# Three column groups of the second token group's right parts are made beside the last attention blocks, kept in DRAM and loaded past the branch

## The chip, the cores and the metric

The kernel runs on one core of one Trainium2 chip. The core has five engines that run their own instruction lists in order and wait for each other through semaphores: TensorE (PE, matmuls; PEld is its weight load), VectorE (DVE), ScalarE (ACT), GpSimd (POOL) and SyncE (SP), which here issues every DMA. The metric is device time in microseconds (us) for one execution of the whole program.

## The reference, cut to what matters

One decoder layer over 2048 tokens of width 1024: a modulated input goes through one projection; half of the heads do sparse attention (an indexer picks 256 causal keys for each query), the other half a gated short convolution; both are normalised, concatenated and multiplied with `w_out`; a residual and a LayerNorm follow. Then the feed-forward part, in which this change lies:

```python
def swiglu(h, w_gate, w_up, w_down):
    return (jax.nn.silu(h @ w_gate) * (h @ w_up)) @ w_down

    x = layer_norm(DEEPNORM_ALPHA * x + g1[:, None, :] * mix, ln1_g[l], ln1_b[l])
    ff = swiglu(modulate(x, sh2, sc2), w_gate[l], w_up[l], w_down[l])
    x = layer_norm(DEEPNORM_ALPHA * x + g2[:, None, :] * ff, ln2_g[l], ln2_b[l])
```

`w_gate` and `w_up` are 1024 x 2816, `w_down` 2816 x 1024. The output is 2048 x 1024, float32.

## The kernel before

**Attention.** The 2048 tokens are 16 blocks of 128. `attention` takes them in the order `ORDER = [2, 4, 7, 0, 10, 1, 9, 3, 8, 5, 6, 11, 13, 12, 15, 14]`. A block of number b has b + 1 steps. In each step TensorE makes two 128 x 512 banks of logits (L888 to L890), ScalarE turns each into `p32` and `ph` (L894, L895), GpSimd makes the remainder `pr = p32 - ph` in two pieces (L897), and two steps later TensorE multiplies `ph` and `pr` with the values (L907 to L909). When a block is done, `finish` normalises it and `mix` multiplies it with `w_out` (L947), normalises (`z`, L951 to L957), stores `z` as `xn_d`, transposes it (L965), scales it into `h2` (L968) and stores that as `h2_d`; the steps of `mix` are spread over the following block. A background generator gets one call in each step.

**The feed-forward product** uses Strassen's scheme with seven products, m = 1, 2, 6, 5, 7, 3, 4 (`HM`), in this order. Each product needs a right part (of the tokens, `HT[grp][m]`) and a left part (of the weights). Tokens are two groups, blocks 0 to 7 and 8 to 15. A right part of a group has four column groups i = 0 to 3; column group i comes from blocks 8 grp + i and 8 grp + 4 + i. `prep_h(grp)` makes them: for each i it loads four 256 KB pieces `hr` of `h2_d`, forms the seven combinations (`right`, L1102 to L1114), and splits each into a float16 high part on ScalarE (L1170) and a low part on VectorE or GpSimd (L1171). For group 1 the combinations of m = 7, 5, 6 and the low parts of m = 7, 5, 6, 4 are VectorE's; the combination of m = 4 and the low parts of m = 1, 2, 3 are GpSimd's.

**What lies where.** `late_topk`, then the weights of pair 0 (`prep_w(0, W0, ...)`) and `prep_h(0)` run as the background of the attention; four of the seven parts of group 0 go through a ring of two tiles (`outs`) to DRAM (`t_d`) and are loaded as the attention's buffers come free (L1295). At the attention's end `head` runs products m = 1, 2, 6, 5 of group 0, pair 0. Then all engines pass a branch (L1348, L1349): a flag made on the chip decides whether a general top-k and the whole attention are done again; on these inputs they are not. Behind the branch: the last left parts of pair 0 (m = 4), products 7, 3, 4 of group 0, and, called after the first of these, `second = prep_h(1)` in full. Then group 1, pair 0, whose product m = 1 needs `HT[1][1]` with all four column groups; then ten more pairs, and the down product.

The framework's scheduler decides, from its own estimate of times, in which order the instructions of each engine stand. SP's list is in order too: a store that waits holds back every DMA behind it.

Of the kernel before, what the change touches and what calls it, by code (L numbers as in the profile page):

```python
# [3 lines left out]

# [8 lines left out]
F16 = mybir.dt.float16  # L13
# [8 lines left out]
P = 128  # L22
# [5 lines left out]
CH = 512  # L28
# [34 lines left out]
ORDER = [2, 4, 7, 0, 10, 1, 9, 3, 8, 5, 6, 11, 13, 12, 15, 14]  # L63
# [7 lines left out]
HM = (1, 2, 6, 5, 7, 3, 4)  # L71
# [71 lines left out]
def body(ctx: ExitStack, tc: tile.TileContext, A, out, force=False):  # L143
    nc = tc.nc
    V, S_, G, T = nc.vector, nc.scalar, nc.gpsimd, nc.tensor
    dma = nc.sync.dma_start

    def dram(name, shape, dt):
        pool = ctx.enter_context(tc.tile_pool(name="d_" + name, bufs=1, space=DRAM))
        return pool.tile(shape, dt, name=name)  # L150
# [6 lines left out]
    xn_d = [dram(f"xn_d{b}", [P, D], F32) for b in range(NB)]  # L157
    h2_d = [dram(f"h2_d{b}", [P, KT * P], F32) for b in range(NB)]
    t_d = {m: dram(f"t_d{m}", [P, 2, 4, CH], F16) for m in HM[3:]}
    g_d2 = [{m: dram(f"gg_d{g}_{m}", [P, 4, NP, 2, P], F16) for m in HM} for g in range(2)]  # L160


# [636 lines left out]


    wo = [], []

    def out_weights(pool):
        for x, tag in ((0, "hi"), (1, "lo")):
# [16 lines left out]
    def attention(pool=None, background=None, at_block=None, at_end=None):  # L821
# [104 lines left out]
        def mix(b, on, x, mc):  # L926
            yield
            pt = mbank()
            for k in range(4):
                T.transpose(pt[:, k * P:(k + 1) * P], on[:, 2 * k:2 * k + 2].rearrange("p h d -> p (h d)"), ident)  # L930
            ah = ap.tile([P, 4, P], F16, tag="ah", name=f"ah{b}", bufs=two)
            al = ap.tile([P, 4, P], F16, tag="al", name=f"al{b}", bufs=two)
            p4 = pt.rearrange("p (k t) -> p k t", t=P)
            S_.activation(ah, p4, AF.Copy)
            V.tensor_tensor(al, p4, ah, op=ALU.subtract)
            yield
            z = ap.tile([P, D], F32, tag="z", name=f"z{b}", bufs=1)
            st = ap.tile([P, 2, 6], F32, tag="st", name=f"st{b}", bufs=2)
            for hh in range(2):
                ns = slice(hh * CH, (hh + 1) * CH)  # L940
                ps = mbank()
                n = 0
                for k in (4, 5, 6, 7, 0, 1, 2, 3):
                    hi = ah[:, k] if k < 4 else mc[:, k - 4, 0]
                    lo = al[:, k] if k < 4 else mc[:, k - 4, 1]
                    for a, w in ((hi, wo[0]), (hi, wo[1]), (lo, wo[0])):
                        T.matmul(ps, a, w[k // 4][:, k % 4, ns], start=n == 0, stop=n == 3 * KT - 1)  # L947
                        n += 1
                    if k % 2:
                        yield  # L950
                V.scalar_tensor_tensor(z[:, ns], x[:, ns], ALPHA * WS, ps, op0=ALU.mult, op1=ALU.add)  # L951
                V.bn_stats(st[:, hh], z[:, ns])
            mv = ap.tile([P, 2], F32, tag="mv", name=f"mvl{b}", bufs=2)
            V.bn_aggr(mv, st.rearrange("p a b -> p (a b)"))
            rs = ap.tile([P, 1], F32, tag="rs", name=f"rs{b}", bufs=2)
            root(ap, rs, mv[:, 1:2], 1.0, EPS * WS * WS)
            V.tensor_scalar(z, z, mv[:, 0:1], rs, op0=ALU.subtract, op1=ALU.mult)  # L957
            dma(xn_d[b], z)
            yield
            yield  # L960
            h2 = ap.tile([P, KT, P], F32, tag="h2", name=f"h2_{b}", bufs=1)
            for hh in range(2):
                ps = mbank()
                for k in range(4):
                    T.transpose(ps[:, k * P:(k + 1) * P], z[:, (hh * 4 + k) * P:(hh * 4 + k + 1) * P], ident)  # L965
                for k in range(4):
                    kk = hh * 4 + k
                    S_.activation(h2[:, kk], ps[:, k * P:(k + 1) * P], AF.Identity, scale=sa[:, kk:kk + 1],  # L968
                                  bias=sb[:, kk:kk + 1])
                yield  # L970
            dma(h2_d[b], h2.rearrange("p k t -> p (k t)"))
            yield

        MIXN = 15
# [42 lines left out]
        for i in range(len(steps) + lag):  # L1017
            if i < len(steps):
                p, b, kt = steps[i]
                left = b - kt  # L1020
                if kt == 0:
# [9 lines left out]
                    x = ap.tile([P, D], F32, tag="x", name=f"x{b}", bufs=keep)  # L1031
# [12 lines left out]
            if i < len(steps):  # L1044
# [3 lines left out]
                if near is not None:  # L1048
# [3 lines left out]
                    k = min(n, near[1]) if near[0] is not None else 0  # L1052
# [19 lines left out]
            pass  # L1072
        at.close()

    late = [None]
    ff = ctx.enter_context(ExitStack())

# [37 lines left out]
    RIGHT = (1, 7, 5, 6, 2, 4, 3)  # L1115
# [33 lines left out]

    HT = [{}, {}]  # L1150

    def prep_h(grp):

        for i in range(4):
            b = []
            for k in range(2):
                for t in range(2):
                    x = raws(f"hr{grp}{i}{t}{k}")
                    dma(x, h2_d[grp * 8 + t * 4 + i][:, k * CH:(k + 1) * CH])
                    b.append(x)  # L1160
            y = sums(f"yh{grp}{i}")
            for m in RIGHT:
                x = right(V if grp and m in H1V else G, b, y, m)
                kept = HT[grp].get(m)
                if kept is None:
                    o = outs(f"ht{grp}{i}_{m}").rearrange("p a x t -> p (a x t)").rearrange("p (x n) -> p x n", x=2)
                    hi, lo = o[:, 0], o[:, 1]
                else:
                    hi, lo = (kept[:, z, i].rearrange("p k t -> p (k t)") for z in range(2))
                S_.activation(hi, x, AF.Copy)  # L1170
                (G if grp and m in H1G else V).tensor_tensor(lo, x, hi, op=ALU.subtract)  # L1171
                if kept is None:
                    dma(t_d[m][:, :, i], o)
                yield

    def held_h(pool, grp, ms):
# [108 lines left out]
    def unsettled(bank_):  # L1285
        for _ in ahead:
            pass
        heads["u"] = [temps(f"u{x}") for x in range(2)]
        heads["g"] = prods("g11")
        held_h(early_h[0].enter_context(tc.tile_pool(name="fel", bufs=1, side="right", reuse_waits="tile")), 0, HM[3:])  # L1290
        few = few_s.enter_context(tc.tile_pool(name="few", bufs=1, side="right", reuse_waits="tile"))
        heads["v"] = [few.tile([P, CH], F32, name=f"v{x}") for x in range(2)]
        wring.add(few, 4)
        for m in HM[3:]:
            dma(HT[0][m].rearrange("p x a k t -> p (x a k t)"), t_d[m].rearrange("p x a n -> p (x a n)"))  # L1295
        for _ in prep_w(0, W0, (7, 3), ((0, 0), (1, 0), (1, 1)), {3: (0, 1)}):
            pass
        heads["c"] = heads["g"], sums("c11")
        return flags(bank_)
# [13 lines left out]
    for t in range(4):  # L1313
        for c in range(NCH):
            if c == 1 and t < 3:
                wcs.append(load_wc(t + 1, wca if t % 2 else vp, lambda: vp.tile([P, CH], F32, tag="cr", name="cr", bufs=3)))
            g = conv(c, t, *hts[c], *wcs[t])
            for j in range(3):
                if (t, c, j) == EARLY_ATT:
                    pull(100000)  # L1320
                    scoring.close()
                    a0 = tks.enter_context(tc.tile_pool(name="a0", bufs=1, side="right", reuse_waits="tile"))
                    tc_ = tks.enter_context(tc.tile_pool(name="tc_", bufs=1, side="right", reuse_waits="tile"))
                    late[0] = late_topk(tc_)
                    ahead = after_late()
                    att = attention(a0, ahead, at_block, unsettled)
                    next(att)
                    weights = out_weights(a0)
                    for _ in weights:
                        pass  # L1330
                next(g)
                if j == 0 and prev is not None:
                    for _ in prev:
                        pass
                pull(PULL)
                next(ada, None)
            prev = g
# [5 lines left out]
    front.close()  # L1343
    for _ in att:
        pass


    rv = nc.values_load(fi[0:1, 0:1], min_val=0, max_val=1)  # L1348
    with tc.If(rv > 0):  # L1349
        general_topk(tc, A, s_d, u_d)  # L1350
        for _ in attention():
            pass
        for _ in prep_h(0):
            pass
        with tc.tile_pool(name="ps2", bufs=1, space=PSUM) as ps2:
            for _ in head(lambda: ps2.tile([P, CH], F32, tag="f", name="f", bufs=4)):
                pass
# [10 lines left out]
    held_h(fp, 1, HM)  # L1368
    for r, n in ((wring, 2), (raws, 2), (sums, 2), (temps, 6), (prods, 4), (outs, 4)):
        r.add(fp, n)  # L1370
    for _ in prep_w(0, W0, (4,), ((1, 1),)):
        pass
    Ws = W0
# [35 lines left out]
    fo = [None]  # L1409
    gpool = [None]  # L1410
    pwd = prep_wd()
    second = prep_h(1)
    for p in range(NP):
        nxt = {}
        pw = prep_w(p + 1, nxt) if p + 1 < NP else iter(())
# [90 lines left out]
    for q in range(8):  # L1506
# [11 lines left out]
        for m in HM:  # L1518
# [18 lines left out]
            k = {2: 0, 7: 3, 3: 1, 4: 2}.get(m)  # L1537
            if k is not None:
                b, hh = blocks[k // 2], k % 2
                if (q, m) != (7, 4):  # L1540
                    x = residual(b, hh)
# [93 lines left out]
```

## Time and profile before

| | |
|---|---|
| median of the three runs | 2543.98 us (2542.55 to 2549.05) |
| the profiled execution | 2544.64 us, of which the trace's span is 2542.8 us |
| PE busy | 2319.4 us, 91% of the span |
| DVE, ACT, POOL busy | 1804.2, 1185.0 and 1230.5 us |
| granted TensorE clock, mean | 0.962 of full speed |

Read the span as stages: projections, indexer and convolution to about 900 us, the attention to about 1240, the end of the attention with `head` to the branch at about 1266, the feed-forward pairs from 1269 to 2073, the down product to the end. An engine's busy time beside a wait of another engine in the same stretch says who sets the pace there; a busy share over the whole span does not.

### The profile page before, as it was taken

To read this page: it belongs to the slowest core of one execution; us is meant where nothing else is said; L and a number is where in the kernel's file an instruction comes from. 1 tells how busy PE (TensorE), PEld (TensorE's weight loads), DVE (VectorE), ACT (ScalarE), POOL (GpSimd) and SP (SyncE) were. 2 spreads that over 40 slices of the span, in tenths; PEclk is the share of its full clock that TensorE was granted. 3 is DMA by queue.
4 is the path that set the end of the run, shared out by engine and by line. 5 is a ranking of instruction groups with operands and counts; after the bars stand their busy time and mean duration, and the time that the engine had idled before them with its cause. 6 is when DMAs were issued, how large, how long until landed. Compare 5 with 4: busy or idle time off the path is not lost.

```text
span 2542.8 us, 38397 instructions
## 1 busy us (share of the span) xinstructions
PE 2319.4 (91%) x13538; PEld 1119.3 (44%) x13538; DVE 1804.2 (71%) x3649; ACT 1185.0 (47%) x2263; POOL 1230.5 (48%) x1232
## 2 busy tenths in 40 slices
PE   5799999996879699889969999999999986999998
PEld 3444444443444355555424444444444432444443
DVE  8998999989999876763396666776666697422223
ACT  3687776646767566777543233332333343110000
POOL 3000000003655666898376556655655565855455
PEclk9799999998989899999979999999999998999999
DMA  8421442434131322330242223222222236444443
GB/s 272 127 104 68 149 133 89 150 123 144 58 121 60 126 93 81 117 110 29 106 132 88 75 87 92 84 71 75 71 88 79 85 115 207 150 141 148 128 137 121
DMA packets 213917, 281.72 MB, mean 111 GB/s; under 512 B 15825, under 2 KB 128849, under 8 KB 212945
## 3 DMA queue, kind: packets, MB, share of 16 engines
q1 hardware_dynamic: 213712, 279.17, 34.5%
q8 instruction: 107, 1.75, 0.3%
q14 instruction: 98, 0.79, 0.1%
HBM read 183.20 MB, written 95.91 MB: 110 GB/s over the span
## 4 chain that ended last, share of the span: by engine, by line
PE 35%; POOL 6%; DMA 4%; DVE 3%; issue 2%; ACT 0%; SPq 0%; DVEq 0%; POOLq 0%
PE f L1207 30%; PE f L1503 5%; DMA x<-xn_d 2%; POOL z L1480 1%; DMA gi<-gg_d 1%; POOL x L1491 1%; POOL x L1490 1%; POOL z L1547 1%; POOL z L1548 1%; DMA wd<-in_wd 1%; DVE wdo L216 0%; DVE h L1171 0%; DVE z L1536 0%; POOL wd L1112 0%; POOL yd L1105 0%
## 5 line engine op out<-in xcount | busy, mean ns | idle before, releaser
L897 POOL TENSOR_TENSOR pr<-p,ph 128x256 f16<-128x256 f32 x544 | 379.6, 730 | 140.2 <-ACT ph L895 61.2
L1207 PE MATMUL f<-h,wwg 128*128 128x512 f16 x1800 | 419.9, 383 | 25.0 <-ACT h L1170 18.0
L1207 PE MATMUL f<-h,wwu 128*128 128x512 f16 x1800 | 414.1, 380 | 0.0
L1241 POOL TENSOR_TENSOR go<-g,go 128x512 f16<-128x512 f32 x126 | 169.7, 1356 | 274.1 <-ACT go L1240 236.3
L1503 PEld LDWEIGHTS <-gi 128*128 128x128 f16 x1848 | 180.7, 99 | 276.2 <-DMA gi<-gg_d 47.4
L1207 PEld LDWEIGHTS <-wwg 128*128 128x128 f16 x1848 | 182.1, 99 | 232.3 <-issue 14.9
L1207 PEld LDWEIGHTS <-wwu 128*128 128x128 f16 x1848 | 181.1, 98 | 234.2 <-issue 17.0
L1503 PE MATMUL f<-wdo,gi 128*128 128x512 f16 x1032 | 242.1, 386 | 15.6 <-DMA gi<-gg_d 6.8
L865 DVE CUSTOM_DVE_ANT_0 jk<-m,ua 128x512 bf16<-128x512 f32 (+3 forms) x320 | 193.7, 605 | 56.2 <-PE m L863 41.6
L894 ACT ACTIVATE p<-l 128x512 f32<-128x512 f32 x272 | 158.3, 598 | 90.7 <-PE l L890 69.2
L1240 ACT ACTIVATE go<-g 128x512 f16<-128x512 f32 x132 | 82.5, 627 | 230.6 <-issue 82.8
L447 ACT ACTIVATE r<-xs 128x512 f32<-128x512 f32 (+3 forms) x304 | 153.4, 548 | 57.3 <-PE xs L446 14.0
L895 ACT ACTIVATE ph<-p 128x512 f16<-128x512 f32 x272 | 166.5, 635 | 2.9
L909 PE MATMUL o<-vst,pr 128*128 128x65 f16 x1088 | 140.4, 196 | 14.4 <-POOL pr L897 13.7
L1503 PE MATMUL f<-wdr,gi 128*128 128x512 f16 x576 | 136.5, 386 | 16.2 <-DMA gi<-gg_d 16.1
L737 PE MATMUL b<-hi,wch 128*128 128x512 f16 x384 | 146.7, 382 | 0.0
L737 PE MATMUL b<-lo,wch 128*128 128x512 f16 x384 | 146.3, 381 | 0.0
L737 PE MATMUL b<-hi,wcl 128*128 128x512 f16 x384 | 146.3, 381 | 0.0
L907 PE MATMUL o<-vst,ph 128*128 128x65 f16 x1088 | 142.8, 194 | 1.8 <-ACT ph L895 1.8
L908 PE MATMUL o<-vst,ph 128*128 128x64 f16 x1088 | 141.5, 194 | 0.0
L1470 ACT ACTIVATE frs<-fmv,epsw 128x1 f32<-128x1 f32 x16 | 4.7, 294 | 282.3 <-DVE fmv L1467 282.3
L863 PE MATMUL m<-k1T,qst 128*128 128x512 f16 (+3 forms) x320 | 105.4, 360 | 29.5 <-DVE mp L865 26.0
(384 smaller groups left out, 5194.3 us busy)
## 6 DMA issues: line engine op xcount, KB each, us to landing
gg_d<-go SPq DMA_DIRECT2D x154, 256.0 KB, 2.6
gi<-gg_d SPq DMA_DIRECT2D x112, 256.0 KB, 3.0
wa<-in_w_ada SPq DMA_DIRECT2D x64, 256.0 KB, 2.9
wg<-in_wg SPq DMA_DIRECT2D x49, 256.0 KB, 3.0
wu<-in_wu SPq DMA_DIRECT2D x49, 256.0 KB, 3.0
wd<-in_wd SPq DMA_DIRECT2D x44, 256.0 KB, 3.0
gi<-gg_d SPq DMA_DIRECT2D x56, 192.0 KB, 2.8
wa<-in_w_ada SPq DMA_DIRECT2D x16, 512.0 KB, 8.6
```

The lines of the kernel that those rows point to most:

```text
L447: S_.activation(r[:, i:i + e], ps[:, 0:e], AF.Relu)
L737: T.matmul(ps, w[:, k, j * P:(j + 1) * P], x[:, k], start=n == 0, stop=n == 3 * KT - 1)
L865: V.tensor_tensor_reduce(jk[:, 0:w], ps[:, 0:w], u[:, j * 512:j * 512 + w], scale=1.0, scalar=-3e38, op0=ALU.add, op1=ALU.max, accum_out=m ...
L894: S_.activation(p32, pl_, AF.Exp, scale=DH ** -0.5)
L895: S_.activation(ph, p32, AF.Copy)
L897: G.tensor_tensor(pr[:, i:i + CH // 2], p32[:, i:i + CH // 2], ph[:, i:i + CH // 2], op=ALU.subtract)
L907: T.matmul(o, lhs, vst[:, kt, 64:129], start=kt == 0 and hh == 0, stop=False)
L908: T.matmul(o[:, 0:64], lhs, vst[:, kt, 0:64], start=False, stop=False)
L909: T.matmul(o, pr[:, hh * P:(hh + 1) * P], vst[:, kt, 64:129], start=False, stop=kt == b and hh == 3)
L1207: T.matmul(ps, w[:, x, k * P:(k + 1) * P], h[:, y, :, k], start=n == 0, stop=n == 11)
L1241: (V if (p, grp) in LASTG else G).tensor_tensor(o[:, :, 1], x4, o[:, :, 0], op=ALU.subtract)
L1503: T.matmul(ps, g[:, p - p0, x], wd_tiles[m, p][:, y], start=p == 0 and n == 0, stop=p == NP - 1 and n == 2)
```

## The change

`prep_h` takes the list of column groups that it makes. A generator `other = prep_h(1, H1PARTS)` with `H1PARTS = [1, 0, 3]` joins the attention's background behind the first one. A set `mixed` holds the blocks whose `h2` has been stored; a column group is begun only when both of its blocks are in it. The seven parts of each go through the two tiles of `outs` to new DRAM tensors `t1_d`. What is begun when the attention ends is finished there, and the rest of `other` is put ahead of the branch. Behind the branch 21 DMAs (three column groups of seven parts, 256 KB each) load them into `HT[1]`, ahead of everything else on SP; `second` makes column group 2 alone (blocks 10 and 14).

```diff
+    t1_d = {m: dram(f"t1_d{m}", [P, 2, 4, CH], F16) for m in HM}
...
+    mixed = set()
+    begun = [False]
...
             dma(h2_d[b], h2.rearrange("p k t -> p (k t)"))
+            mixed.add(b)
...
+    H1PARTS = [i for i in (1, 0, 3, 2) if ORDER[-1] % 4 != i]
...
-    def prep_h(grp):
-
-        for i in range(4):
+    def prep_h(grp, parts=range(4)):
+
+        for i in parts:
+            while not {grp * 8 + i, grp * 8 + 4 + i} <= mixed:
+                yield
+            begun[0] = True
...
                 (G if grp and m in H1G else V).tensor_tensor(lo, x, hi, op=ALU.subtract)
+                begun[0] = m != RIGHT[-1]
                 if kept is None:
-                    dma(t_d[m][:, :, i], o)
+                    dma((t1_d if grp else t_d)[m][:, :, i], o)
...
     def unsettled(bank_):
         for _ in ahead:
             pass
+        while begun[0]:
+            next(other)
...
-                    att = attention(a0, ahead, at_block, unsettled)
+                    other = prep_h(1, H1PARTS)
+                    att = attention(a0, chain(ahead, other), at_block, unsettled)
...
     for _ in att:
         pass
+    for _ in other:
+        pass
...
+    for m in HM:
+        for i in H1PARTS:
+            dma(HT[1][m][:, :, i].rearrange("p x k t -> p x (k t)"), t1_d[m][:, :, i])
     for _ in prep_w(0, W0, (4,), ((1, 1),)):
         pass
...
-    second = prep_h(1)
+    second = prep_h(1, [i for i in range(4) if i not in H1PARTS])
```

How this moves instructions is seen in three places. Line numbers of the changed program are a few higher (L897 is L901, L1105 to L1112 are L1111 to L1118, L1171 is L1180, L1093 to L1099 are L1099 to L1105).

First GpSimd in the last attention block, 14: `pr` is the attention's remainder, `wg` and `wu` the weights of pair 0, `ht` a right part on its way to DRAM, `hr` a loaded piece of `h2`. Before:

```order
L897 TENSOR_TENSOR pr<-p_16426,ph 128x256 x2
L897 TENSOR_TENSOR pr<-p_16437,ph 128x256 x2
L897 TENSOR_TENSOR pr<-p_16483,ph 128x256 x2
L897 TENSOR_TENSOR pr<-p_16494,ph 128x256 x2
L897 TENSOR_TENSOR pr<-p_16540,ph 128x256 x2
```

In the change:

```order
L901 TENSOR_TENSOR pr<-p_16458,ph 128x256 x2
L1099 TENSOR_TENSOR wg_00_17209<-wg_00_17209,wg_10_17213 128x512
L1180 TENSOR_TENSOR ht_2_17177<-hr_17075,ht_2_17177 128x512
L901 TENSOR_TENSOR pr<-p_16504,ph 128x256 x2
L1118 TENSOR_TENSOR hr_17075<-hr_17075,hr_17071 128x512
L901 TENSOR_TENSOR pr<-p_16515,ph 128x256 x2
L1099 TENSOR_TENSOR wu_00_17211<-wu_00_17211,wu_10_17215 128x512
L901 TENSOR_TENSOR pr<-p_16561,ph 128x256 x2
L901 TENSOR_TENSOR pr<-p_16572,ph 128x256 x2
L1180 TENSOR_TENSOR ht_3_17186<-hr_17077,ht_3_17186 128x512
L1100 TENSOR_TENSOR ywg_17221<-wg_11_17217,wg_00_17209 128x512
```

Six combinations of weights (two each of L1099, L1100, L1105) that stood ahead of block 15 and four pieces of right parts now stand between the remainders of ten banks; from the first of these ten operations to the end of the attention 20 banks of remainders follow, with nothing between them before.

Second ScalarE at the end of `mix` of block 14, the last work ahead of the branch; `h_14` is that block's `h2`. Before:

```order
L793 ACTIVATE rw<-mvl_17309,epsw 128x1
L794 ACTIVATE ry<-rw 128x1
L968 ACTIVATE h_14_17323<-m,sb,sa 128x128
L968 ACTIVATE h_14_17323<-m,sb,sa 128x128 x3
```

In the change:

```order
L796 ACTIVATE ry<-rw 128x1
L1179 ACTIVATE ht_7_17491<-yh_17485 128x512
L1179 ACTIVATE ht_5_17496<-hr_17479 128x512
L1179 ACTIVATE ht_6_17501<-hr_17477 128x512
L972 ACTIVATE h_14_17426<-m,sb,sa 128x128
L972 ACTIVATE h_14_17426<-m,sb,sa 128x128 x3
L972 ACTIVATE h_14_17426<-m,sb,sa 128x128
L972 ACTIVATE h_14_17426<-m,sb,sa 128x128 x3
L1179 ACTIVATE ht_2_17505<-hr_17481 128x512
L1179 ACTIVATE ht_4_17510<-hr_17481 128x512
L1179 ACTIVATE ht_3_17514<-hr_17483 128x512
```

Six of the seven parts of column group 3 (blocks 11 and 15) now stand around the last `h2`; VectorE and GpSimd have their low parts and combinations there too.

Third SP's list behind the branch. Before:

```order
L1349 UNCONDITIONAL_BRANCH x2
L1120 DMA wg_11_29453<-in_wg 128x512
L1120 DMA wu_11_29455<-in_wu 128x512
L1159 DMA hr_29490<-h_d_321 128x512
L1159 DMA hr_29492<-h_d_333 128x512
```

In the change:

```order
L1390 DMA h_1_29713<-t_d_357 128x2x512 x3
L1390 DMA h_2_29714<-t_d_360 128x2x512 x3
L1390 DMA h_6_29715<-t_d_363 128x2x512 x3
L1390 DMA h_5_29716<-t_d_366 128x2x512 x3
L1390 DMA h_7_29717<-t_d_369 128x2x512 x3
L1390 DMA h_3_29718<-t_d_372 128x2x512 x3
L1390 DMA h_4_29719<-t_d_375 128x2x512 x3
L1126 DMA wg_11_29741<-in_wg 128x512
L1126 DMA wu_11_29743<-in_wu 128x512
```

The two weight pieces for m = 4 (`wg_11`, `wu_11`) stood first and now stand behind the 21 loads; the four `hr` of column group 2 follow them.

## Rows read from the trace of the kernel before

**Rows 1.** Windows: stretch, length, busy us (instructions) by engine, clock, DMA share, GB/s

```profile
1070.00:1100.00 30.00, 24.64 (x248) 13.35 (x246) 25.81 (x46) 22.90 (x46) 30.00 (x35) 1.00 0.54 167
1100.00:1130.00 30.00, 29.42 (x294) 16.97 (x295) 20.21 (x55) 18.76 (x37) 29.84 (x40) 1.00 0.25 84
1150.00:1180.00 30.00, 30.00 (x316) 17.09 (x315) 11.30 (x32) 20.82 (x37) 25.23 (x39) 1.00 0.01 2
1205.50:1235.70 30.20, 29.66 (x333) 17.56 (x332) 5.73 (x11) 23.99 (x46) 24.56 (x38) 1.00 0.12 41
...
1286.50:1301.80 15.30, 0.05 (x1) 0.00 (x0) 15.30 (x17) 6.79 (x11) 11.77 (x8) 0.61 0.29 90
...
1329.60:1400.00 70.40, 70.40 (x327) 31.91 (x326) 46.65 (x54) 22.42 (x39) 45.36 (x34) 1.00 0.26 83
```

**Rows 2.** Timeline of PE: start, us, what, idle before it and its releaser

```profile
1242.55 0.60 PE L930 MATMUL m<-ct,on 128*128 128x128 f32 x4
...
1269.15 4.45 PE L1207 MATMUL f<-h,wwg 128*128 128x512 f16 x12 [3.64 <-DVEq L1349]
1273.43 2.75 PE L1207 MATMUL f<-h,wwu 128*128 128x512 f16 x12
1276.02 2.75 PE L1207 MATMUL f<-h,wwg 128*128 128x512 f16 x12
...
1301.85 0.59 PE L1207 MATMUL f<-h,wwg 128*128 128x512 f16 x1 [15.30 <-ACT h L1170]
...
1321.53 4.85 PE L1207 MATMUL f<-h,wwg 128*128 128x512 f16 x11 [3.30 <-DVE h L1171]
1326.17 3.42 PE L1207 MATMUL f<-h,wwu 128*128 128x512 f16 x12
1329.43 2.75 PE L1207 MATMUL f<-h,wwg 128*128 128x512 f16 x12
```

**Rows 3.** Chain of work that ended last: start, us, what

```profile
1321.53 751.41 PE f L1207 x3467
```

**Rows 4.** Timelines of POOL, DVE, ACT and SP around the branch

```profile
1234.37 1.30 POOL L897 TENSOR_TENSOR pr<-p,ph 128x256 f16<-128x256 f32 x2 [1.24 <-issue]
...
1258.36 0.81 DVE L957 TENSOR_SCALAR z<-z,mvl,rs 128x1024 f32<-128x1024 f32 x1
...
1259.93 2.91 ACT L968 ACTIVATE h<-m,sb,sa 128x128 f32<-128x128 f32 x8 [2.18 <-PE m L965]
...
1262.86 0.32 SPq L971 DMA_DIRECT2D h_d<-h  x1
...
1265.54 0.69 DVE L1234 TENSOR_TENSOR v<-m,u 128x512 f32<-128x512 f32 x1 [1.90 <-PE m L1207]
...
1269.23 0.34 SPq L1120 DMA_DIRECT2D wg<-in_wg  x1
```

**Rows 5.** Tiles of prep_h: operation and count, ns min/median/max; DMA landing

```profile
L1171 POOL TENSOR_TENSOR h<-hr,h x12: 1155/1482/1603, 1276.0 to 1314.8; 128x512 f16<-128x512 f32 x12
...
L1105 DVE TENSOR_TENSOR yh<-hr,hr x4: 678/1596/1757, 1278.8 to 1310.5; 128x512 f32<-128x512 f32 x4
...
L1173 SPq DMA_DIRECT2D t_d<-ht x12: 513/524/559, 1024.7 to 1101.6; - x12
...
DMA to landing us min/median/max: 2.4/2.9/5.5
```

**Rows 6.** Timeline of POOL: the first two of six combinations of weights

```profile
1094.62 1.26 POOL L1093 TENSOR_TENSOR wg<-wg,wg 128x512 f32<-128x512 f32 x1
1100.97 1.72 POOL L1093 TENSOR_TENSOR wu<-wu,wu 128x512 f32<-128x512 f32 x1
```

**Rows 7.** Timeline of ACT in the attention: one high part of group 0

```profile
1083.95 0.63 ACT L1170 ACTIVATE ht<-yh 128x512 f16<-128x512 f32 x1 [3.42 <-DMA t_d<-ht]
```

**Rows 8.** DMA totals of two stretches, 2 to 30 us and 1269 to 1278 us

```profile
DMA packets 8214, 9.76 MB, mean 348 GB/s; under 512 B 430, under 2 KB 7031, under 8 KB 8214
...
DMA packets 1297, 2.32 MB, mean 258 GB/s; under 512 B 131, under 2 KB 185, under 8 KB 1295
```

More of the change, by code (lines that the diff above doesn't have):

```diff
@@ L2 @@
 from contextlib import ExitStack
+from itertools import chain
 from statistics import NormalDist
@@ L1353, in body @@
         for _ in prep_h(0):
+            pass
+        for _ in prep_h(1, H1PARTS):
             pass
```

## The prediction

> **What bounds the kernel now.** I read three things in this order: busy times by stretch, the timeline of TensorE around the branch, and the chain that ended last.
>
> In the last attention blocks TensorE sets the pace and GpSimd is close behind: in the last 30.2 us PE is busy 29.66, POOL 24.56 and ACT 23.99 [rows 1]. Earlier, while the weights of pair 0 are prepared, POOL is the full one (30.00 of 30 and 29.84 of 30) and PE has room once [rows 1].
>
> Behind the branch TensorE starts at 1269.15 and runs six blocks (products 7, 3, 4 of group 0): the first takes 4.28 to the next start, the others 2.59 each [rows 2], so they end at 1269.15 + 4.28 + 5 x 2.59 = 1286.4. Then it stands still for 15.30 us, released by a high part on ACT [rows 2]. In that gap VectorE is busy all 15.30 us, and TensorE's granted clock averages 0.61 (a mean between 2.4 GHz, full speed, and 1.2) [rows 1]: `prep_h(1)` is VectorE-bound, and TensorE waits for all four column groups. A shorter wait (3.30) ends at 1321.53 [rows 2]. From there the last chain is one piece of 751 us of PE alone [rows 3], busy 70.40 of 70.40 us [rows 1]. So time saved or lost ahead of about 1329 goes through to the end, and I cost everything up to the end of the twelfth block behind the branch (product 6, group 1), at 1329.43 [rows 2].
>
> **Behind the branch: a gain.** Before, it is 1329.43 - 1269.15 = 60.3 us from TensorE's start to that point [rows 2]. In the change 21 loads of 256 KB stand on SP ahead of the two weight pieces of product 4. Products 7 and 3 don't need them: 4.28 + 3 x 2.59 = 12.05 us. Product 4 must wait for the 23rd load. At 348 GB/s, the rate in the opening stretch [rows 8], a load takes 0.753 us, 23 take 17.3, and the shortest landing of 2.4 less its own 0.75 adds 1.65 [rows 5]: 19.0 us past the merge. Then a high part on ACT (0.63 [rows 7]) and a low part on VectorE (nearest: the shortest 128x512 combination, 0.68 [rows 5]): product 4 starts at 20.3, after a gap of 8 us in place of 15.3. Its two blocks cost about 8.0 us as behind the earlier wait (1321.53 to 1329.43 [rows 2]), then six more at 2.59 (15.5): 43.8 us. The gain is 16.5.
> - Lower bound: the loads run at the 258 GB/s seen right behind the branch [rows 8]: 25.0 us to landing, gain 10.5.
> - Upper bound: SP's issue is the limit, 23 x 0.559 + 2.9 = 15.8 us [rows 5], gain 19.7. I take 348: these loads too are a row of large transfers with nothing between them.
> - Column group 2 itself (about a fourth of the old VectorE work) follows its four `hr` behind the 23 loads, near 23 us; product 1 of group 1 isn't due before 28. I cost it at nothing; if the loads come late, both move together.
>
> The Trainium skill, page "DMA: Bandwidth & Descriptors", section Bandwidth, advises to batch transfers to 1 MiB, and between its 64 KB and 1 MB rows I estimate 2.0 us for 256 KB; one after the other, 23 would land at 46 us and the term turn from +16.5 to -10.5. The opening stretch (9.76 MB at 348 GB/s [rows 8]) speaks against it, as several transfers lie in flight there; the sum goes by the rows.
>
> **Ahead of the branch: a loss.** Column group 3 needs blocks 11 and 15, so six of its seven parts now stand in the tail of `mix` 14. Before, `z` starts at 1258.36, the scaling of `h2` at 1259.93 for 2.91 us, its store is issued at 1262.86, VectorE's last piece ends at 1266.23 and the merge is 2.92 later [rows 4]. After:
> - VectorE has some five more pieces (0.68 each at best [rows 5], 3.4 us) and ACT three high parts ahead of the scaling. Most lies under TensorE's product 6; I take the transposes 1.3 us later, so the scaling ends at 1264.1.
> - Then `ht_2`: high part 0.63 [rows 7], low part on POOL about 1.3 [rows 5]: 1266.1. Its store lands 2.9 later [rows 5], 1269.1. `outs` has two tiles, so `ht_3` waits for that landing: 0.63 and 1.3 more give 1271.0, and its store is issued by 1271.5.
> - The merge 2.9 later: 1274.4. If it also waits for that store to land, up to 1277.6. I take 1275.7: a loss of 6.5 (5.3 to 8.4). Unlike the work behind the branch, this has no matmul to hide under.
>
> **In the attention: a loss.** POOL gets the work.
> - Last block: ten operations (six weight combinations, four parts) move in between the remainders. At 1.27 each (weights 1.26 and 1.72 [rows 6], low parts from 1.155 [rows 5]) that is 12.7 us; POOL has 30.20 - 24.56 = 5.6 idle [rows 1]. So 7 us of overflow; at 1.72 it is 17.2 and 11.6. If the remainders tighten, whose present mean is 24.56 / 38 = 0.65 us [rows 1], it is less: 4 if each of 38 saves 0.08.
> - Relief: the six combinations and others leave the stretch where POOL is full (1070 to 1130): up to five of 1.27, but PE has room only in part there (24.64 and 29.42 of 30 [rows 1]): -2 (0 to -5).
> - Column group 1's four POOL operations (5.1 us) come where POOL has 4.8 idle (25.23 of 30 [rows 1]): 0.5 (0 to 3).
> - High parts that wait for the `outs` ring: the one seen waited 3.42 us [rows 7]; ACT has 6.2 idle in the last block [rows 1], so 1 (0 to 3.4).
> - VectorE's share (5.73 of 30.2 busy in the last block [rows 1]) and SP's stores (0.52 each [rows 5]) have cover many times over; nothing.
> Together a loss of 6.5 (from a gain of 1 to a loss of 18). The end of the attention itself is a fixed row of steps: the last remainder ends at 1235.67 [rows 4], L930 starts at 1242.55 [rows 2].
>
> **Sum.** 16.5 - 6.5 - 6.5 = 3.5 gained. The profiled execution took 2544.64, 0.66 over the median of 2543.98: 2541.1 as a profile, 2540.5 as a median. The order of the down stage also shifts a little (3 either way at most is my guess); nothing.
>
> **Rivals.**
> - **A, POOL has room.** The remainders can run closer together, the last block costs nothing (7 less), and the merge comes at its early bound (1.2 less): 2532. For it: a remainder is needed two steps later only (L907 to L909), and ACT has 6.2 idle there, so POOL may be paced from outside. Against it: 12.7 us into 5.6 idle. Chance 0.25.
> - **B, POOL at its slow price.** All its operations at 1.72 [rows 6], no relief, and part 1 costs 3: the attention loses 15.6, the kernel 5.6: 2549.6. For it: VectorE is busier in the same stretches now, and of the two prices in rows 6 the second was dear. Against it: half of the low parts took 1.48 or less [rows 5]. Chance 0.13.
> - **C, the ring of two stalls ScalarE: slower.** Place: the attention steps in which column groups 1 and 0 are made. ACT stands still for a store (3.42 us [rows 7]) while `ph` of the next bank waits behind it, and TensorE behind that. Of the fourteen high parts five uncovered ones cost 17, 16 more than I took: 2556.6. It is slower by over 0.3% from the fourth such wait on. For it: that wait stands in the trace, and PE has no room in 1150 to 1180 (30.00 of 30 [rows 1]). Against it: a part comes only once in some steps, and a store lands in 2.9. Chance 0.08.
> - **D, the loads don't overlap.** 23 at 2.4 each [rows 5] land at 55 us, 36 later: 2577. Against it: 348 GB/s and 258 GB/s in rows 8. The skill's table on the page named above would give, by the estimate there, some 2567. Chance 0.04.
>
> **How the numbers follow.** The forecast has 0.50, A 0.25, B 0.13, C 0.08, D 0.04. Three tenths of a per cent is 7.6 us, about what the measurement tells from no change. Faster by more: A and a tenth of the forecast's own spread, 0.30. Slower by more: C and D, 0.12. Within: 0.58. The range takes in A with the loads at their upper bound (2532 - 3 = 2529) and B with the merge at its late bound (2549.6 + 1.9, 2552), and leaves out C, D and a little below: 2529 to 2552. The forecast's own range is 2534 to 2547.
>
> **What would show it.** Behind the branch: one gap on PE of about 8 us, ended by product 4's part, where 15.3 stood; the last of the 23 loads about 19 us past the merge; no other gap over 2 us. Ahead: the merge about 6.5 us later, counted from L930, with two low parts on POOL behind the last `h2`. In the attention: POOL above 95% in the last block, the block some 7 us longer, PE's waits there ended by `pr`. If POOL is full and the block is not longer, A holds; if PE's waits are ended by `ph` behind an ACT wait for a store, C does. The prediction is wrong if L930 comes earlier than before or more than 12 us later, or if the gap for product 4 is over 15 us.

## The result, and the profile after

The changed kernel took 2557.9 us (median of six runs, 2552.81 to 2565.19) against 2544.2 for the kernel before (2540.61 to 2549.05): ratio 1.0054, 95% interval 1.0036 to 1.0072, so about 14 us slower. The prediction was 2540.5 (2529 to 2552), and "slower by over 0.3%" had a chance of 0.12. The profiled execution is the shortest of the six, 2552.81 us with a span of 2551.0, 8.2 over the span before; the 14 us are the medians' difference.

Four stretches hold the difference (`on` is a block's normalised output, ahead of `mix`). They run from the transposes of `on` of block 12 to those of block 15 ("block 15"), from there to those of block 14 ("block 14"), from there to TensorE's first matmul behind the branch ("the tail"), and from there to the end of the twelfth block of 12 matmuls. Their windows in the kernel before, in this order (columns as in [rows 1], engines in the order PE, PEld, DVE, ACT, POOL):

```profile
1147.29:1196.48 49.19, 46.09 (x517) 27.39 (x513) 21.39 (x53) 39.42 (x79) 39.82 (x60) 1.00 0.09 34
1196.48:1242.55 46.07, 45.53 (x477) 26.39 (x478) 9.87 (x22) 33.07 (x64) 32.19 (x50) 1.00 0.22 82
1242.55:1269.15 26.60, 22.42 (x110) 10.57 (x108) 10.60 (x20) 4.02 (x12) 0.00 (x0) 1.00 0.26 101
1269.15:1329.43 60.28, 38.94 (x145) 15.84 (x146) 56.01 (x55) 29.73 (x50) 40.74 (x28) 0.75 0.44 140
```

And in the changed kernel:

```profile
1147.58:1204.80 57.22, 49.19 (x538) 28.81 (x534) 31.21 (x65) 44.94 (x90) 51.89 (x69) 1.00 0.31 106
1204.80:1266.86 62.06, 48.91 (x456) 27.27 (x457) 21.15 (x27) 33.46 (x65) 41.75 (x55) 0.89 0.35 118
1266.86:1297.77 30.91, 23.80 (x108) 11.32 (x109) 13.93 (x26) 8.25 (x19) 3.57 (x3) 0.94 0.43 159
1297.77:1345.80 48.03, 36.66 (x145) 15.22 (x144) 26.91 (x31) 16.95 (x28) 24.47 (x18) 0.80 0.70 226
```

The attention loses 8.0 us in the stretch of block 15 and 16.0 in that of block 14, the tail loses 4.3, and behind the branch 12.3 come back: 16.1 lost by the twelfth block, 16.4 with the 0.3 that the first window starts later. TensorE's last matmul of the pairs also starts 16.4 later (2089.13 against 2072.76). The down stage of this one execution then gives 8.2 back. From the start of that last block of matmuls to the end it is 461.9 to 467.2 us in the ten profiles of kernels with the change, and 470.0 and 468.6 in the two without it, so part of the gain probably comes with the change; why is not shown.

The largest single piece is on TensorE in block 14. Timeline of the changed kernel, TensorE's wait for block 15's `z` and its two waits behind the branch:

```profile
1240.78 1.11 PE L969 MATMUL m<-ct,z 128*128 128x128 f32 x4 [8.78 <-DVE z L961]
...
1297.77 5.28 PE L1217 MATMUL f<-h,wwg 128*128 128x512 f16 x12 [5.90 <-ACTq L1364]
...
1322.59 1.04 PE L1217 MATMUL f<-h,wwg 128*128 128x512 f16 x2 [11.37 <-ACT wwg L217]
```

VectorE ahead of that `z`, same kernel:

```profile
1230.50 8.98 DVE L798 TENSOR_TENSOR rw<-ry 128x1 f32<-128x1 f32 x1 [2.35 <-ACT ry L796]
1239.52 0.16 DVE L799 TENSOR_TENSOR rw<-rw,rv 128x1 f32<-128x1 f32 x1
1239.71 0.16 DVE L800 SCALAR_TENSOR_TENSOR rs<-rw,ry 128x1 f32<-128x1 f32 x1
1239.90 0.81 DVE L961 TENSOR_SCALAR z<-z,mvl,rs 128x1024 f32<-128x1024 f32 x1
```

A product of two columns of 128 numbers took 8.98 us; the next one like it took 0.16. Now GpSimd in the same time:

```profile
1230.83 1.27 POOL L1105 TENSOR_TENSOR wu<-wu,ywu 128x512 f32<-128x512 f32 x1
1232.05 1.30 POOL L901 TENSOR_TENSOR pr<-p,ph 128x256 f16<-128x256 f32 x2
1233.30 1.16 POOL L1180 TENSOR_TENSOR ht<-hr,ht 128x512 f16<-128x512 f32 x1
1234.41 5.05 POOL L901 TENSOR_TENSOR pr<-p,ph 128x256 f16<-128x256 f32 x8
1246.10 1.30 POOL L901 TENSOR_TENSOR pr<-p,ph 128x256 f16<-128x256 f32 x2 [6.64 <-issue]
```

GpSimd runs without a break to 1234.41 + 5.05 = 1239.46; VectorE's product ends at 1239.48. The transposes of `z` stand ahead of attention steps in TensorE's order, so TensorE stands 8.78 us, its clock falls (0.89 in the mean of the stretch, between 2.4 and 1.2 GHz), and GpSimd itself then stands 6.64 us. The profile names no releaser for that; ScalarE, which feeds it, stands until 1241.93 for the same transposes and has the next bank ready at 1245.97.

All of TensorE's waits in block 14 (us in total, times, longest; the row of `on` also holds the wait of 3.12 that ends block 15):

```profile
PE m L969 <- DVE z L961: 8.8, 1, 8.8
PE m L934 <- DVE on L927: 7.0, 2, 3.8
PE l L892 <- ACT p L898: 0.4, 2, 0.3
```

None is for a remainder. The 16.0 us are 8.2 more for `z`, 3.9 more for `on`, and 3.4 more of TensorE's own busy time, with 21 matmuls fewer and at the lower clock.

The Trainium skill, page "SBUF — State Buffer", section "Who interferes with whom", has a rule for it: a VectorE instruction with two operands in SBUF and a GpSimd instruction that reads SBUF exclude each other, and the one that comes second waits for the whole other instruction. The rows agree on the kind of instruction but not on the length: one GpSimd instruction took 0.63 to 1.3 us, and this wait outlasted twelve.

Behind the branch the new wait is the chain of waits' own (pieces in order of time):

```profile
1304.18 5.76 DMA h<-t_d
...
1309.96 5.96 DMA h<-t_d
...
1315.98 5.84 DMA wg<-in_wg
...
1321.91 0.64 ACT wwg L217
```

This chain carries TensorE's wait for product 4: SP issues the weight piece only at 1315.98, behind the 21 loads.

### The profile page after: what moved, and what is told of

The parts are those of the page before. It is cut to its first block, busy times and chain, and to the rows that moved or that the text cites. A ratio compares the mean times of both kernels' runs of the same rounds, so it can differ in the third digit from the quotient of the medians.

```text
span 2551.0 us, 38500 instructions
## 1 busy us (share of the span) xinstructions
PE 2320.4 (91%) x13538; PEld 1122.7 (44%) x13538; DVE 1802.2 (71%) x3649; ACT 1182.1 (46%) x2263; POOL 1227.8 (48%) x1232
## 5 line engine op out<-in xcount | busy, mean ns | idle before, releaser
L901 POOL TENSOR_TENSOR pr<-p,ph 128x256 f16<-128x256 f32 x544 | 385.3, 739 | 148.9 <-ACT ph L899 64.7
```

The source lines that it names most:

```text
L901: G.tensor_tensor(pr[:, i:i + CH // 2], p32[:, i:i + CH // 2], ph[:, i:i + CH // 2], op=ALU.subtract)
```

## The experiments

Every kernel below differs from the changed kernel by its edit, except the control. The table gathers the four stretches (us, from each profile) and the ratio to the kernel before, run beside it; the text follows.

| kernel | block 15 | block 14 | tail | 12 blocks | sum | ratio (95%) |
|---|---|---|---|---|---|---|
| before | 49.2 | 46.1 | 26.6 | 60.3 | 182.1 | 1 |
| changed | 57.2 | 62.1 | 30.9 | 48.0 | 198.2 | 1.0054 (1.0036 to 1.0072) |
| act_norm15 | 56.6 | 52.0 | 33.0 | 46.8 | 188.5 | 1.0009 (0.9999 to 1.0018) |
| no_pool | 57.4 | 49.4 | 31.7 | 44.3 | 182.9 | 0.9990 (0.9981 to 1.0000) |
| w_first | 58.1 | 62.7 | 31.3 | 44.2 | 196.2 | 1.0042 (1.0029 to 1.0055) |
| parts_1 | 63.1 | 46.2 | 26.6 | 51.0 | 186.9 | 1.0009 (1.0000 to 1.0017) |
| hr_first | 57.6 | 62.5 | 31.1 | 32.4 | 183.7 | 0.9998 (0.9989 to 1.0008) |
| all3 | 58.0 | 48.0 | 31.6 | 34.0 | 171.6 | 0.9957 (0.9945 to 0.9969) |
| all3_parts_10 | 59.2 | 47.9 | 28.4 | 44.3 | 179.7 | 0.9996 (0.9986 to 1.0006) |
| no_pool_hr_first | 61.1 | 47.8 | 31.7 | 33.6 | 174.2 | 0.9933 (0.9919 to 0.9947) |

My theory after the result was S: VectorE is starved by a GpSimd that never pauses. The rival was P, the prediction's own term: GpSimd simply has too much to do in that block.

**act_norm15.** Block 15's normalisation goes to ScalarE.

```diff
-            root(ap, rs, mv[:, 1:2], 1.0, EPS * WS * WS)
-            V.tensor_scalar(z, z, mv[:, 0:1], rs, op0=ALU.subtract, op1=ALU.mult)
+            if pool is not None and b == ORDER[-2]:
+                S_.activation(w, mv[:, 1:2], AF.Ln, bias=epsw)
...
+                S_.activation(rs, n0, AF.Identity, scale=y, bias=y3)
...
+                S_.activation(z, z, AF.Identity, scale=rs, bias=n1)
```

> The changed kernel with one edit: the normalisation in mix of block 15 (the small root steps and the scaling of z) is done by ScalarE instead of VectorE; the output is the same in value. Theory S (starved VectorE): in the changed kernel VectorE's 128x1 product of two SBUF tensors took 8.98 us because GpSimd ran without a break to the same instant, and TensorE stood 8.78 us at the transposes behind it. Then here the stall ahead of these transposes falls below 2 us, the end of the last block (the transposes of on) comes 6 to 9 us earlier after block 15's, and the median is 5 to 9 us below the changed kernel's (ratio to before 1.002 to 1.0035). Theory P (GpSimd is simply too full in that block: ten more operations of 1.27 us): the stall goes, but TensorE waits for remainders instead; the end of the last block moves by less than 2 us and the median stays within 3 us of the changed kernel's.

TensorE ahead of the transposes of `z`:

```profile
1233.30 1.09 PE L982 MATMUL m<-ct,z 128*128 128x128 f32 x8 [1.24 <-ACT z L971]
```

The wait fell from 8.78 to 1.24, block 14's stretch from 62.1 to 52.0, and the ratio from 1.0054 to 1.0009. S held, with somewhat more than it had forecast, and P did not: with GpSimd's operations unchanged, 10 of the 16 us were gone.

**act_norm15_before**, the control: the same edit in the kernel before.

> Control: the kernel before with the same edit as in the first experiment (normalisation of block 15 on ScalarE). In the kernel before, that 128x1 product took 0.16 us and TensorE waited 0.5 us for z. Theory S: nothing to gain here, within 2 us of the kernel before (ratio 0.9992 to 1.0008). If the edit helps by itself for another reason (VectorE relieved), the time falls by 5 us or more, and the first experiment shows nothing about the stall.

Ratio 1.0005 (0.9997 to 1.0014): nothing gained, so the edit helps only where the stall is. Block 14's stretch was 49.25 there, 3 longer.

**no_pool.** The right parts beside the attention leave GpSimd.

```diff
-                x = right(V if grp and m in H1V else G, b, y, m)
+                x = right(V if grp and (m in H1V or HT[grp].get(m) is None) else G, b, y, m)
...
-                (G if grp and m in H1G else V).tensor_tensor(lo, x, hi, op=ALU.subtract)
+                (G if grp and m in H1G and kept is not None else V).tensor_tensor(lo, x, hi, op=ALU.subtract)
```

> The changed kernel with the right parts that are made beside the attention taken off GpSimd: the combination of product 4 and the low parts of products 1, 2 and 3 are VectorE's there. Theory P: GpSimd has some five operations of 1.27 us fewer in block 15 and four fewer in block 14, so block 15 is about 4 to 6 us shorter, block 14 about 5, and the median 7 to 11 us lower than the changed kernel's. Theory S: VectorE's operations with two SBUF operands wait wherever GpSimd runs without a break; the remainders stay slow (0.73 to 0.75 us), blocks gain 0 to 4 us in all, and the stall ahead of the transposes may stay, since six weight combinations still stand between the remainders.

Block 14 came down to 49.4 and the stall to 1.0 us, more than either theory had. But not because GpSimd paused: the same product of two columns took 0.47 us here in the middle of an unbroken run of 16 remainders (VectorE, then GpSimd):

```profile
1235.95 0.47 DVE L798 TENSOR_TENSOR rw<-ry 128x1 f32<-128x1 f32 x1 [1.43 <-ACT ry L796]
```

```profile
1231.95 10.57 POOL L901 TENSOR_TENSOR pr<-p,ph 128x256 f16<-128x256 f32 x16
```

So S is incomplete: an unbroken GpSimd alone does not make VectorE wait, and why the wait went away here is not shown. Block 15 stayed at 57.4, which P had 4 to 6 us shorter. GpSimd's remainders in block 15's stretch, first in the kernel before, then in the change, then here (mean in ns behind the busy time):

```profile
L897 POOL TENSOR_TENSOR pr<-p,ph 128x256 f16<-128x256 f32 x59 | 38.4, 687 | 9.8 <-issue 8.9 <-POOL pr L897 0.5 <-PE o L909 0.4
```

```profile
L901 POOL TENSOR_TENSOR pr<-p,ph 128x256 f16<-128x256 f32 x64 | 46.0, 751 | 5.8 <-issue 5.5 <-POOL pr L901 0.2
```

```profile
L901 POOL TENSOR_TENSOR pr<-p,ph 128x256 f16<-128x256 f32 x64 | 47.5, 777 | 9.0 <-issue 8.4 <-POOL pr L901 0.6
```

What GpSimd no longer did itself it lost to slower remainders: the busier VectorE is (21.4, 31.2 and 35.1 us in this stretch), the longer one remainder takes (687, 751, 777 ns). So there the two engines slow each other, whichever has the work.

**hi_only**, a test of that. The right parts keep loads, high parts and stores; their combinations and low parts are left out, so the output is not the layer's, and of this single run only the stretches are read.

```diff
+                hi_only = grp and kept is None
...
+                if not hi_only:
+                    (G if grp and m in H1G else V).tensor_tensor(lo, x, hi, op=ALU.subtract)
```

> The changed kernel; the right parts that are made beside the attention keep their loads, their high parts on ScalarE and their stores, but the combinations and the low parts on VectorE and GpSimd are left out (the high part is stored twice), so no VectorE or GpSimd work of theirs lies beside the remainders. The run is read for the length of block 15 (from the transposes of on of block 12 to those of block 15: 49.2 us before, 57.2 in the change, 57.4 without right parts on GpSimd). Contention theory (operations of VectorE and GpSimd on SBUF operands take time from each other, whichever engine has them): 49 to 52 us, remainders at 0.69 us or less, and no stall ahead of the transposes. If ScalarE's seven high parts, the ring of two stores or the order of instructions make the loss: 55 us or more.

```profile
1151.14:1205.48 54.34, 49.37 (x554) 29.23 (x550) 21.93 (x53) 45.38 (x92) 43.61 (x65) 1.00 0.37 125
1205.48:1261.02 55.54, 46.31 (x441) 26.12 (x442) 16.26 (x24) 33.33 (x66) 35.70 (x51) 0.93 0.36 124
```

The remainders were back at 693 ns, with VectorE at 21.9 us. But block 15 took 54.3, between the two, so by this run the left-out work is 2.9 of its 8.0 us; it may be more, as this stretch holds 16 matmuls more than the change's (554 against 538). Some 3 of the 8.0 are no loss but TensorE's order: it is busy 3.1 us more in this stretch, in the change much as here, with 21 matmuls more in the change (538 against 517), and has 21 fewer in block 14's. TensorE's waits name most of the rest. Before, then in the change, for `on` (at the end of the stretch) and for remainders:

```profile
1196.48 0.66 PE L930 MATMUL m<-ct,on 128*128 128x128 f32 x4 [0.66 <-DVE on L923]
PE o L909 <- POOL pr L897: 0.4, 1, 0.4
```

```profile
1204.80 1.11 PE L934 MATMUL m<-ct,on 128*128 128x128 f32 x4 [3.12 <-DVE on L927]
PE o L913 <- POOL pr L901: 2.4, 7, 0.7
```

That is 4.5 us more, 2.5 of them for VectorE's `on`: between the steps of `finish` four operations of column group 0 now stand (1198.68 to 1203.04). And the stall was still there, against my expectation: VectorE's product took 6.87 us, TensorE waited 5.50 for `z`. It needs no part on GpSimd; the six weight combinations, which the change pushed from ahead of block 15 into block 14, and a backlog of remainders were there, as they were in no_pool, where the stall was not.

**parts_1.** Column group 1 alone is made beside the attention (`H1PARTS = [1]`).

> The changed kernel with column group 1 alone made beside the attention (groups 0, 3 and 2 past the branch). Seven loads past the branch instead of 21. Theory S and P both: block 14 has no parts between its remainders, so the end of the last block and the branch come back to within 3 us of the kernel before, plus what block 15 costs with column group 1 in it. If column group 1 is what makes block 15 8 us longer, that loss stays; if it is column group 0 (its VectorE operations stand ahead of block 15's own normalisation), block 15 is within 3 us of before. Behind the branch VectorE makes three column groups: of the 15.3 us gap a quarter goes (4 us). Time: 0 to 5 us under the kernel before if the second holds, 3 to 6 us over it if the first does.

Block 14 and the tail came back to before (46.2, 26.6). Block 15 took 63.1, with a second case of the same stall in it, now in `finish`. VectorE, then GpSimd:

```profile
1203.56 6.86 DVE L920 TENSOR_TENSOR asq<-ov 128x512 f32<-128x512 f32 x1 [16.18 <-ACT ov L917]
```

```profile
1192.21 17.65 POOL L901 TENSOR_TENSOR pr<-p,ph 128x256 f16<-128x256 f32 x28
```

GpSimd's 28 remainders run from 1192.21 to 1209.86; VectorE's square of `ov` ends at 1210.42, half a us behind them; ScalarE's root waits for it, and TensorE waits 5.59 us for ScalarE's step behind that. Without that wait block 15 is 57.5, 8 longer than before with no column group 0 in it. That is not column group 1 alone, though: the six weight combinations, which stand in block 14 in the change, stand in block 15 here (GpSimd, the first and the last):

```profile
1169.43 1.27 POOL L1099 TENSOR_TENSOR wg<-wg,wg 128x512 f32<-128x512 f32 x1 [0.16 <-PE l L894]
1190.98 1.27 POOL L1105 TENSOR_TENSOR wu<-wu,ywu 128x512 f32<-128x512 f32 x1
```

So the run does not decide between my two alternatives. TensorE's wait for `on` is 0.29 us here, in line with column group 0's part in it. The ratio is 1.0009, some 2 us over the kernel before, where the first had 3 to 6.

**w_first.** The two weight pieces of product 4 are loaded ahead of the 21 right parts.

```diff
+    for _ in prep_w(0, W0, (4,), ((1, 1),)):
+        pass
     for m in HM:
         for i in H1PARTS:
             dma(HT[1][m][:, :, i].rearrange("p x k t -> p x (k t)"), t1_d[m][:, :, i])
-    for _ in prep_w(0, W0, (4,), ((1, 1),)):
-        pass
```

> The changed kernel with the two weight pieces of product 4 loaded ahead of the 21 right parts. The step of the prediction: product 4 waited 11.37 us only because its weights stand behind 21 loads. If that is all, the gap goes and the time falls by 8 to 11 us. Rival: the wait moves on. The four pieces hr of column group 2 still stand behind the 23 loads; in the changed kernel they landed about 28 us after the branch, and product 1 of group 1 would now be due at about 17. Then TensorE waits there 8 to 11 us, and the time falls by 0 to 3 us.

TensorE's first matmul of product 1, group 1:

```profile
1329.37 0.59 PE L1217 MATMUL f<-h,wwg 128*128 128x512 f16 x1 [9.92 <-ACT h L1179]
```

The rival held: 11.37 us for product 4 turned into 9.92 for product 1, since column group 2's four `hr` still stood behind 23 loads. The twelve blocks took 44.2 in place of 48.0.

**hr_first.** The four `hr` go ahead of the loads as well.

```diff
+    second = prep_h(1, [i for i in range(4) if i not in H1PARTS])
+    next(second)
     for m in HM:
         for i in H1PARTS:
```

> The changed kernel with another order of loads behind the branch: the two weight pieces of product 4, the four pieces hr of column group 2, then the 21 right parts. Theory: both waits behind the branch (11.37 us for product 4 in the changed kernel, 9.92 us for product 1 of group 1 with the weights alone first) come from what stands behind 21 loads on SP, so here neither is over 3 us, the twelve blocks behind the branch take 33 to 38 us in place of 48.0, and the median falls by 9 to 14 us below the changed kernel's. Rival: VectorE needs its time for column group 2 anyway, or the 21 loads, now last, are waited for by products 1 and 2; then the wait moves on once more and the gain is under 5 us.

```profile
1301.16:1333.58 32.42, 32.42 (x145) 14.40 (x145) 22.23 (x27) 14.46 (x24) 18.19 (x13) 0.96 0.94 308
```

TensorE is busy 32.42 of 32.42 us. 27.9 us are gained behind the branch in place of 12.3, and the kernel comes level with before (0.9998) with the attention's loss still in it; the product of two columns took 9.00 us again.

**all3**, the three edits together, and **all3_parts_10**, the same with column groups 1 and 0 alone.

> The changed kernel with the three edits together: block 15's normalisation on ScalarE, no right parts on GpSimd beside the attention, weights and hr ahead of the 21 loads. Sum of the parts: blocks 15 and 14 some 11 us longer than in the kernel before, the tail to the branch some 5 longer, the twelve blocks behind it 33 to 38 us in place of 60.3, so 6 to 12 us under the kernel before (ratio 0.9953 to 0.9976). If the loss in block 15 comes from the edits' own VectorE work it stays at 8 us; GpSimd's remainders there then stay at 0.75 us or more against 0.687 before.

> As the one before, but with column groups 1 and 0 alone made beside the attention, 3 and 2 past the branch. The step of the prediction that column group 3 costs the tail 6.5 us: then the stretch from the last transposes of on to the branch comes back to 26 to 28 us (31 to 33 with it). Behind the branch VectorE makes two column groups in place of one: the twelve blocks take 0 to 8 us more than with one. Sum: the same as the one before to 5 us less, if the two work in the cover of products 7, 3 and 4; up to 5 us more if not.

All three: 0.9957, as the sum had it. With two column groups the tail came down from 31.6 to 28.4, but behind the branch VectorE had two groups to make, TensorE waited 5.98 us for product 1, and the twelve blocks took 10.3 us more, over the 8 that I had allowed; by the medians it is 10.5 us slower than with three, where I had 5 at most.

**no_pool_hr_first**, the version with two edits.

> The changed kernel with two edits only: no right parts on GpSimd beside the attention, and weights and hr ahead of the 21 loads; block 15's normalisation stays on VectorE. Without right parts on GpSimd the stall ahead of the transposes had been 1.0 us, so the third edit should bring nothing any more: as the version with three edits, 0 to 3 us under it (the third edit cost the kernel before 1 us), ratio to before 0.994 to 0.9965. If the stall comes back, 0.998 or more.

2531.0 us, ratio 0.9933 (0.9919 to 0.9947), a little under the 0.994 that I had as the lowest: the best one, faster than both kernels. The third edit brought nothing here, as expected; if anything it costs. Its last two stretches:

```profile
1258.25:1289.97 31.72, 24.15 (x109) 11.31 (x109) 15.79 (x29) 7.69 (x18) 0.00 (x0) 0.92 0.42 157
1289.97:1323.58 33.61, 33.61 (x144) 14.71 (x145) 24.64 (x29) 16.93 (x28) 21.65 (x17) 0.92 0.99 326
```

The stretches explain 8 of its 17 us, the down stage another 4 (465.9 against 470.0); the rest lies in stages that I did not take apart.

## Why the prediction was wrong

**The attention term failed.** It stood at 6.5 us, with 18 as its far end, and was 24; L930 (L934 in the change) came 24.3 us later, and over 12 was to show the prediction wrong. Its path failed, not only its size. I added up GpSimd's busy time against its idle time, let TensorE wait for late remainders, and set VectorE's share at nothing, because VectorE is idle most of the block ("cover many times over"). In the last block, 7 in the sum and 16.0 in the trace, TensorE waited for no remainder at all, and GpSimd was not over 95% busy but 41.75 us of 62.06: the waits were for VectorE's `z` and `on`. Block 15, 0.5 in the sum, lost 8.0. The relief of 2 did not come: from the transposes of `on` at 1054 to the start of block 15 it took 93.5 us, and 93.3 before, though GpSimd was busy 5.9 us less.

Two things were missing. VectorE's idle time is not free where GpSimd works on SBUF: the remainders slowed from 687 to 751 ns, and `on` came late behind column group 0's operations (together 2.9 of block 15's 8.0 us by hi_only, 4.5 by TensorE's waits). And one tiny VectorE instruction on the way to `z` can stand for as long as GpSimd runs on. act_norm15 shows what that cost: 10 us.

In the rows before, a hint stood: small operations of one kind took 0.16 and 0.58 us within one block, beside remainders (VectorE in block 14 of the kernel before):

```profile
1226.36 0.16 DVE L796 TENSOR_TENSOR rw<-ry 128x1 f32<-128x1 f32 x1 [1.55 <-ACT ry L794]
1226.55 0.58 DVE L797 TENSOR_TENSOR rw<-rw,rv 128x1 f32<-128x1 f32 x1
1227.16 0.59 DVE L798 SCALAR_TENSOR_TENSOR rs<-rw,ry 128x1 f32<-128x1 f32 x1
```

[rows 5] has another: one 128x512 combination took 678 to 1757 ns on VectorE, and the sum used the shortest.

**The tail** cost 4.3 where 6.5 stood (5.3 to 8.4), under its range. Its mechanism was right: two low parts on GpSimd stand behind the last `h2` (1290.12 and 1294.75), the last store is issued 29.1 us behind the transposes of `on` (1295.93), 29.0 in the sum, and all3_parts_10, without column group 3, took 28.4 in place of 31.6. The size was not: TensorE was past the branch 1.84 us after that issue, where the sum had over 4.

**Behind the branch** 12.3 came where 16.5 stood, inside its bounds. The gap was 11.37, not 8: the loads started 3.1 us behind TensorE (1300.90), and the last weight piece was there 24 past the merge, not 19.0. That TensorE would find the new wait at product 4 was right. That the order of the loads, not their number, cost 16 us more I had not seen: with `hr` first the same loads hide altogether. Column group 2, which I cost at nothing, came out so only because both waits lay on top of each other: w_first took one away and the other stood there. The down stage, at nothing in the sum (3 either way at most), gave 8.2 back in the profile; without that the forecast would lie further off.

**The rivals.** C had 2556.6, near the measured time, by luck: ScalarE's waits for the two-tile ring were 2.8 us in blocks 15 and 14 together, not 17. B's dear price was not seen on the moved operations (1.15 to 1.3 us, one at 1.72), but on the remainders. D fell: the 21 loads and the first weight piece landed within 21 us. A fell with the forecast.

## What to carry to other kernels

An engine's idle time is cover only if its instructions don't need what a busy engine holds: before work goes into VectorE's or GpSimd's idle time, look in the trace for instructions of the same form with two durations, and for the small ones on the way to TensorE. An engine near full that loses its last breaks can cost more than the overflow says, through what waits for a break; a sum of busy times does not show it. Where a change sends a row of loads past a point, order them by who waits first: here the order was worth as much as the change cost.

## What the runs showed of the hardware

- Some of VectorE's instructions with two SBUF operands waited until GpSimd's unbroken run ended: 8.98, 8.96 and 9.00 us in three kernels at the same place, 6.87 there in hi_only, 6.86 at another place in parts_1. Elsewhere VectorE got in between, in no_pool even at the same place (0.47), and with block 12's normalisation in the changed kernel (VectorE, then GpSimd):

```profile
1183.19 0.57 DVE L798 TENSOR_TENSOR rw<-ry 128x1 f32<-128x1 f32 x1 [2.03 <-ACT ry L796]
```

```profile
1179.30 27.69 POOL L901 TENSOR_TENSOR pr<-p,ph 128x256 f16<-128x256 f32 x38
```

There a remainder took 27.69 / 38 = 0.73 us; beside the long waits the remainders took 0.63, their fastest pace in these traces, which may as well follow from VectorE's standing still. What decides between the two was not settled.
- With 21 loads of 256 KB in a row each landed in 5.9 us (median), where the stores of [rows 5] took 2.9, and SP took 14.80 us to issue them, 0.70 each against 0.52. DMA issues and SP in the changed kernel:

```profile
h<-t_d SPq DMA_DIRECT2D x21, 256.0 KB, 5.9
```

```profile
1300.90 14.80 SPq L1390 DMA_DIRECT2D h<-t_d  x21
```
